# Last output blocks of each sublayer: four blocks per token half at a time, in place of two

## The chip, the cores and the metric

The kernel runs on one core of a Trainium2 chip. The metric is the device time of one execution in microseconds; the time before is the median of three runs.

## The reference, cut to what matters

One inference step through two trunk layers, for 512 prompt tokens and 64 sample tokens that share all weights. Each layer has three sublayers: an FFN, a mixer, an FFN. Each sublayer normalises its input, ends in a matrix product onto 1024 outputs, normalises that, and adds it to the residual stream.

```python
def swiglu(x, w_gate, w_up, w_down):
    return (jax.nn.silu(x @ w_gate) * (x @ w_up)) @ w_down
...
        x = x + 0.5 * rmsnorm(swiglu(rmsnorm(x, g[0]), ffn_gate[li, 0], ffn_up[li, 0], ffn_down[li, 0]), g[1])
        h = rmsnorm(x, g[2])
...
        x = x + rmsnorm(y, g[3])
        x = x + 0.5 * rmsnorm(swiglu(rmsnorm(x, g[4]), ffn_gate[li, 1], ffn_up[li, 1], ffn_down[li, 1]), g[5])
```

The mixers are a gated DeltaNet beside a short convolution (even layer) and sparse attention beside a gating MLP (odd layer); both end in one output projection. A norm needs a sum over all 1024 outputs of a token, so a sublayer's result can be normalised for a token only when all of that token's output blocks are there.

## The kernel before, in words

Activations lie transposed: 128 features on the partitions, KC = 8 chunks of features, tokens along the free axis. The 576 tokens are split in two halves, half 0 with 256 columns and half 1 with 320 (`HW`). Every product is done in three passes (`mm3`): high part of the weight by high part of the activation, high by low, low by high. A weight tile is loaded by SP's queue (`raw`), its high part is cast by ACT (`whi`) and its low part subtracted on DVE (`wlo`); tiles rotate in a pool `wp` of four. TensorE (PE) is the engine that the layout is built for.

**The end of a sublayer.** `ffn` (its second part) and `proj_out` make eight output blocks `mb` for each half `hf`. A block of an FFN is 33 matmuls (11 chunks, three passes), one of an output projection 24. `self.out_order` sets their order: blocks 0 to 5 for half 0 and half 1 in turn, then blocks 6 and 7 for half 0, then 6 and 7 for half 1. When half 0 has its last block, `boundary` is called for it, and later for half 1.

**The boundary.** It has a chain of its own. The sum of squares of y (`acc`, kind y) is summed over partitions by two or three one-column matmuls (L161); ACT takes a root (L163), DVE a reciprocal (L167), PE spreads it by a transpose (L173). Then DVE scales y (L234, `bt`) and adds it to the residual x (L236, L238), ACT and DVE write the high and low part of the next sublayer's operand (L202 `xh`, L203 `xl`), ACT squares x (L186) and POOL adds the squares up (L187, `acc`, kind x). From that `acc` a second round of L161, L163, L167, L173 makes the next sublayer's pre-norm factor r. For half 0 that second round is written straight into the boundary; for half 1 it is put off (`later`) until the last chunk of the next sublayer's first group.

**The next sublayer.** Its first group has four weight tiles. `group` does all four for half 0, tile by tile, then all four for half 1 chunk by chunk. PSUM has five banks for them (three `g`, two `f`), so half 1 needs banks that DVE must first have emptied of half 0's results (in an FFN L316 and L317, tiles t and u; in the mixers L433, L472 and others).

**What sets the order.** The code records operations; a scheduler orders each engine's queue by its own estimate of times. At run time each engine takes its queue in that order, so an instruction that waits holds all behind it. Tiles of a pool that is opened anew wait for the tiles that lay at their address before (`reuse_waits="tile"`).

Of the kernel before, what the change touches and what calls it, by code (L numbers as in the profile page):

```python
# [8 lines left out]
F32 = mybir.dt.float32  # L9
F32R = mybir.dt.float32r  # L10
# [6 lines left out]
P = 128  # L17
# [6 lines left out]
KC = D // P  # L24
# [9 lines left out]
HW = (256, 320)  # L34
# [4 lines left out]
class Step:  # L39
    def __init__(self, ctx, tc, a, o):  # L40
# [17 lines left out]
        self.small = {}  # L58
        self.out_order = [(mb, hf) for mb in range(KC - 2) for hf in range(2)]
        self.out_order += [(mb, hf) for hf in range(2) for mb in range(KC - 2, KC)]  # L60

# [42 lines left out]

    def weight(self, src, inner=P, pool=None):
        nc = self.nc
        pool = pool or self.wp
        shape = [P, 8 * P // inner, inner]
        raw = self.wp.tile(shape, F32, tag="raw", name=self.nm("raw"), bufs=3)
        bufs = 4 if pool is self.wp else 2  # L110
        hi = pool.tile(shape, F32R, tag="whi", name=self.nm("whi"), bufs=bufs)
        lo = pool.tile(shape, F32R, tag="wlo", name=self.nm("wlo"), bufs=bufs)
        nc.sync.dma_start(raw, src)
        self.last_split = self.split(hi, lo, raw)
        return hi, lo
# [26 lines left out]
    def behind(self, inst):  # L142

        return self.tc.issue_after(inst.ins) if inst else nullcontext()

    def new_act(self):
        hi, lo = [], []
        for hf in range(2):
            hi.append(self.res.tile([P, KC, HW[hf]], F32R, tag=f"xh{hf}", name=self.nm("xh")))
            lo.append(self.res.tile([P, KC, HW[hf]], F32R, tag=f"xl{hf}", name=self.nm("xl")))  # L150
        return hi, lo

# [131 lines left out]
    def ffn(self, l, f, act, rs, gpost, gnext, first=None):  # L284
        nc, a = self.nc, self.a
        with ExitStack() as ctx:
            hp = ctx.enter_context(self.tc.tile_pool(name=self.nm("ffn"), bufs=1, reuse_waits="tile"))
            yp = ctx.enter_context(self.tc.tile_pool(name=self.nm("y"), bufs=1, side="right", reuse_waits="tile"))
            y = [yp.tile([P, KC, HW[hf]], F32, name=self.nm("y")) for hf in range(2)]
            accy = [None, None]  # L290
            nact, nrs = None, [None, None]
            rs = list(rs)
            hp.tile([P, 16], F32, tag="pad", name=self.nm("pad"))
            for part in range(2):
# [26 lines left out]
                tiles = {}  # L321
                if part == 1:
                    x = self.load_x(yp)
                    if (l, f) == (0, 1):
                        nc.sync.dma_start(self.o["win_past"], a["win"])
                    if (l, f) == (0, 0):
                        self.small_weights()

                def block(n):
                    t = n // 8  # L330
                    if t not in tiles:
                        tiles[t] = self.weight(a["wdn"][l, f, part, t], pool=yp if part == 1 and t >= 9 else None)
                    return tiles[t][0][:, n % 8, :], tiles[t][1][:, n % 8, :]

                for mb, hf in self.out_order:
                        w = HW[hf]
# [6 lines left out]
                        else:  # L343
# [4 lines left out]
                            if mb == KC - 1:  # L348
                                if nact is None and gnext is not None:
                                    nact = self.new_act()  # L350
                                nrs[hf] = self.boundary(hf, y, x, accy[hf], gpost, 0.5, gnext, nact)
# [3 lines left out]
    def proj_out(self, wsrc, oact, order, gpost, gnext):  # L355
        nc = self.nc
        with ExitStack() as ctx:
# [5 lines left out]
            x = self.load_x(hp)  # L363
            for mb, hf in self.out_order:
                    if mb not in ws:
                        ws[mb] = self.weight(wsrc[mb], pool=hp if mb >= KC - 2 else None)
                    whi, wlo = ws[mb]
# [1130 lines left out]
```

## Time and profile before

| | us |
|---|---|
| median of three runs (lowest, highest) | 2471.99 (2470.40, 2478.14) |
| the profiled execution | 2458.22 |
| its span | 2456.2 |
| its mean granted TensorE clock | 0.986 |
| PE busy | 2408.7 (98% of the span) |
| DVE, ACT, POOL busy | 1246.9, 925.6, 185.9 |

A granted clock of 1.00 is TensorE's upper level, 2.4 GHz, and 0.50 the lower, 1.2 GHz. The program has six sublayers in this order: FFN, even mixer, FFN, FFN, odd mixer, FFN; so five boundaries between sublayers and one end. The boundaries lie near 424 us (first, FFN to mixer), 816 (second, mixer to FFN), 1237 (third, FFN to FFN), 1663 (fourth, FFN to mixer) and 2011 (fifth, mixer to FFN).

### The profile page before, as it was taken

The numbers are of one execution on the slowest core, as the hardware profiler recorded it, in microseconds if no ns is written. First come the engines' busy times: TensorE is split into PE (matmuls) and PEld (weight loads), VectorE is DVE, ScalarE is ACT, GpSimd is POOL, SyncE is SP. The second block draws the span as 40 slices with busy tenths as digits, with TensorE's granted clock in tenths as the row PEclk, the third lists the DMA queues.
The fourth block names the chain that finished last, engine by engine and source line by source line (L and its number), as shares of the span: only waits on it lengthen the run. The fifth ranks groups of instructions, "written<-read, shape, count | busy, mean of one in ns | idle before, by whom it ended". The sixth has DMA issues, their size and how long they took to land.

```text
span 2456.2 us, 43363 instructions
## 1 busy us (share of the span) xinstructions
PE 2408.7 (98%) x18169; PEld 2319.2 (94%) x18169; DVE 1246.9 (51%) x2482; ACT 925.6 (38%) x1719; POOL 185.9 (8%) x274
## 2 busy tenths in 40 slices
PE   7999999999999999999999999999999999999998
PEld 7999999898999999999999999999867799999997
DVE  5432443767765654244465424446647646423444
ACT  5322334554423532233353223243346645222332
POOL 3000000400001200000020000004103001000000
PEclk9999999999999999999999999999989999999999
DMA  6222222311214332222233222234502123222221
GB/s 223 83 84 76 97 86 89 108 43 52 68 53 143 112 104 87 86 79 86 95 120 104 78 87 87 86 96 149 177 24 78 57 78 138 86 87 78 86 87 56
DMA packets 70323, 226.72 MB, mean 92 GB/s; under 512 B 11136, under 2 KB 17568, under 8 KB 70096
## 3 DMA queue, kind: packets, MB, share of 16 engines
q1 hardware_dynamic: 64288, 204.27, 24.7%
q0 software_dynamic: 5552, 19.57, 2.4%
q8 instruction: 143, 2.34, 0.4%
q14 instruction: 52, 0.43, 0.1%
q10 hardware_dynamic: 288, 0.11, 0.0%
HBM read 204.26 MB, written 20.72 MB: 92 GB/s over the span
## 4 chain that ended last, share of the span: by engine, by line
PE 76%; issue 17%; DVE 5%; ACT 1%; DMA 1%; POOL 0%; POOLq 0%; SPq 0%; DVEq 0%; ACTq 0%
PE psg L119 14%; PE psg L121 14%; PE psg L120 14%; PE psf L120 8%; PE psf L121 8%; PE psf L119 8%; PE psm L1206 1%; PE psm L494 1%; DVE xl L203 1%; PE psm L516 1%; PE psf L1248 1%; PE psg L1235 1%; PE psm L514 1%; DVE x L236 1%; DVE bt L234 1%
## 5 line engine op out<-in xcount | busy, mean ns | idle before, releaser
L119 PE MATMUL psg<-xh,whi 128*128 128x256 f32 (+1 forms) x2464 | 734.6, 298 | 12.4 <-ACT whi L101 10.2
L120 PE MATMUL psg<-xl,whi 128*128 128x256 f32 (+1 forms) x2464 | 733.9, 298 | 5.1 <-DVE xl L203 4.7
L121 PE MATMUL psg<-xh,wlo 128*128 128x256 f32 (+1 forms) x2464 | 730.7, 297 | 2.2 <-DVE wlo L102 2.1
L102 DVE TENSOR_TENSOR wlo<-raw,whi 128x1024 fp32r<-128x1024 f32 x330 | 405.5, 1230 | 353.1 <-ACT whi L101 351.7
L101 ACT CAST whi<-raw 128x1024 fp32r<-128x1024 f32 x330 | 345.5, 1050 | 554.4 <-PE psg L120 344.9
L119 PEld LDWEIGHTS psg<-xh,whi 128*128 128x128 f32 x2464 | 467.5, 190 | 16.6 <-ACT whi L101 10.5
L120 PEld LDWEIGHTS psg<-xl,whi 128*128 128x128 f32 x2464 | 467.1, 190 | 9.6 <-DVE xl L203 7.7
L121 PEld LDWEIGHTS psg<-xh,wlo 128*128 128x128 f32 x2464 | 467.0, 190 | 4.4 <-DVE wlo L102 2.7
L120 PE MATMUL psf<-xl,whi 128*128 128x320 f32 (+1 forms) x1280 | 376.4, 294 | 1.5 <-DVE xl L203 1.3
L119 PE MATMUL psf<-xh,whi 128*128 128x320 f32 (+1 forms) x1280 | 376.5, 294 | 0.5 <-ACT xh L202 0.3
L121 PE MATMUL psf<-xh,wlo 128*128 128x320 f32 (+1 forms) x1280 | 375.9, 294 | 0.3
L119 PE MATMUL psg<-hh,whi 128*128 128x256 f32 (+1 forms) x836 | 246.0, 294 | 0.0
L120 PE MATMUL psg<-hl,whi 128*128 128x256 f32 (+1 forms) x836 | 245.6, 294 | 0.0
L121 PE MATMUL psg<-hh,wlo 128*128 128x256 f32 (+1 forms) x836 | 245.5, 294 | 0.0
L120 PEld LDWEIGHTS psf<-xl,whi 128*128 128x128 f32 x1280 | 240.7, 188 | 2.6 <-DVE xl L203 2.2
L119 PEld LDWEIGHTS psf<-xh,whi 128*128 128x128 f32 x1280 | 240.9, 188 | 1.2 <-ACT xh L202 0.5
L121 PEld LDWEIGHTS psf<-xh,wlo 128*128 128x128 f32 x1280 | 240.9, 188 | 0.9 <-DVE wlo L102 0.9
L187 POOL TENSOR_TENSOR acc<-acc,sq 128x320 f32<-128x320 f32 (+1 forms) x77 | 70.6, 917 | 1379.8 <-ACT sq L186 1358.8
L119 PE MATMUL psf<-hh,whi 128*128 128x320 f32 (+1 forms) x572 | 169.5, 296 | 0.0
L120 PE MATMUL psf<-hl,whi 128*128 128x320 f32 (+1 forms) x572 | 169.3, 296 | 0.0
L121 PE MATMUL psf<-hh,wlo 128*128 128x320 f32 (+1 forms) x572 | 169.0, 296 | 0.0
L101 ACT CAST hh<-u 128x320 fp32r<-128x320 f32 (+1 forms) x176 | 75.9, 433 | 243.4 <-DVE u L319 243.2
(469 smaller groups left out, 3192.8 us busy)
## 6 DMA issues: line engine op xcount, KB each, us to landing
raw<-in_wgu SPq DMA_DIRECT2D x176, 512.0 KB, 3.3
raw<-in_wdn SPq DMA_DIRECT2D x88, 512.0 KB, 3.3
raw<-in_w_ein SPq DMA_DIRECT2D x28, 512.0 KB, 3.4
raw<-in_w_oin SPq DMA_DIRECT2D x14, 512.0 KB, 3.5
xd<-x SPq DMA_DIRECT2D x10, 640.0 KB, 2.9
x<-xd POOLq DMA_DIRECT2D x10, 640.0 KB, 7.2
xd<-x SPq DMA_DIRECT2D x10, 512.0 KB, 2.7
x<-xd POOLq DMA_DIRECT2D x10, 512.0 KB, 5.0
```

Source lines behind the costliest of these rows:

```text
L101: first = nc.scalar.copy(hi, src)
L102: nc.vector.tensor_tensor(lo, src, hi.bitcast(F32), ALU.subtract)
L119: mm(out, whi, ahi, start=first, stop=False)
L120: mm(out, whi, alo, start=False, stop=False)
L121: mm(out, wlo, ahi, start=False, stop=last)
L187: return (eng or nc.vector).tensor_tensor(acc[:, :w], acc[:, :w], sq[:, :w], ALU.add)
L203: nc.vector.scalar_tensor_tensor(lo, xs, g, hi.bitcast(F32), ALU.mult, ALU.subtract)
L234: nc.vector.tensor_tensor(t, y[hf][:, k:k + n, :], r[:, None, :w].to_broadcast([P, n, w]), ALU.mult)
L236: (nc.gpsimd if gnext is None and hf and k == 0 else nc.vector).tensor_tensor(xs, xs, t, ALU.add)
L494: nc.tensor.matmul(pz[:w, i * w:i * w + w], m[:, i, :], x[:, i, :], start=True, stop=True)
L514: nc.tensor.matmul(pr[:, 1, i, :], xt[:, i, :], zt[:, i, :], start=True, stop=True)
L516: nc.tensor.matmul(pr[:, 0, i, :], zt[:, i, :], xt[:, i, :], start=True, stop=True)
```

## The change

`out_order` becomes a function: blocks 0 to 3 go in turn, then blocks 4 to 7 for one half, then 4 to 7 for the other. In the last sublayer half 1 goes first and half 0 last; elsewhere half 0 goes first. The first part of an FFN, which has no boundary behind it, goes in turn throughout (`in_turn`). The weights of the last four blocks are kept for both halves: in an output projection four tiles in its own pool (two before); in an FFN two in its pool and two in the room of half 1's operand of the sublayer that is ending (`spare`), whose last reader is done by then. Operand tiles are allocated half by half (`half_act`). The FFN's pad grows from 64 to 192 bytes. Line numbers shift: L161 becomes L171, L173 L183, L203 L213, L234 L244, L316 L326, L317 L327.

```diff
-        self.out_order = [(mb, hf) for mb in range(KC - 2) for hf in range(2)]
-        self.out_order += [(mb, hf) for hf in range(2) for mb in range(KC - 2, KC)]
+        self.in_turn = [(mb, hf) for mb in range(KC) for hf in range(2)]
+
+    def out_order(self, last):
+
+        halves = (1, 0) if last else (0, 1)
+        return [(mb, hf) for mb in range(KC - 4) for hf in halves] + [(mb, hf) for hf in halves for mb in range(KC - 4, KC)]
...
-    def weight(self, src, inner=P, pool=None):
+    def weight(self, src, inner=P, pool=None, bufs=2, dst=None):
...
-        bufs = 4 if pool is self.wp else 2
-        hi = pool.tile(shape, F32R, tag="whi", name=self.nm("whi"), bufs=bufs)
-        lo = pool.tile(shape, F32R, tag="wlo", name=self.nm("wlo"), bufs=bufs)
+        if dst:
+            hi, lo = dst
+        else:
+            bufs = bufs if pool else 4
+            hi, lo = [(pool or self.wp).tile(shape, F32R, tag=t, name=self.nm(t), bufs=bufs) for t in ("whi", "wlo")]
...
+    def half_act(self, hf):
+        return [self.res.tile([P, KC, HW[hf]], F32R, tag=f"x{s}{hf}", name=self.nm("x" + s)) for s in "hl"]
+
     def new_act(self):
...
+        return [list(t) for t in zip(*[self.half_act(hf) for hf in range(2)])]
+
+    def spare(self):
+
+        flat = [t.rearrange("p k c -> p (k c)")[:, 16:16 + 2 * KC * P].rearrange("p (i s c) -> p i s c", i=2, c=P)
+                for t in self.half_act(1)]
+        return [[t[:, i] for t in flat] for i in range(2)]
...
-            hp.tile([P, 16], F32, tag="pad", name=self.nm("pad"))
+            hp.tile([P, 48], F32, tag="pad", name=self.nm("pad"))
...
                 if part == 1:
+                    kept = self.spare()
                     x = self.load_x(yp)
...
-                        tiles[t] = self.weight(a["wdn"][l, f, part, t], pool=yp if part == 1 and t >= 9 else None)
+                        pool, dst = None, None
+                        if part == 1 and t >= 7:
+                            pool, dst = (yp, None) if t < 9 else (None, kept[t - 9])
+                        tiles[t] = self.weight(a["wdn"][l, f, part, t], pool=pool, dst=dst)
...
-                for mb, hf in self.out_order:
+                for mb, hf in self.out_order(gnext is None) if part else self.in_turn:
...
-                                if nact is None and gnext is not None:
-                                    nact = self.new_act()
+                                if gnext is not None:
+                                    nact[0][hf], nact[1][hf] = self.half_act(hf)
...
-            for mb, hf in self.out_order:
+            for mb, hf in self.out_order(False):
                     if mb not in ws:
-                        ws[mb] = self.weight(wsrc[mb], pool=hp if mb >= KC - 2 else None)
+                        ws[mb] = self.weight(wsrc[mb], pool=hp if mb >= KC - 4 else None, bufs=4)
```

**Where half 0's second round stands on PE.** The engine is PE, the place the third boundary, FFN to FFN. The `acc` in these rows is half 0's sum of squares of x (kind x). Before, in the next sublayer's first group (`psg` tiles of half 0 by the operand `xh`, `xl`):

```order
L119 MATMUL psg_13351<-xh_13084,whi_13328 128x256
L121 MATMUL psg_13376<-xh_13084,wlo_13335 128x256
L119 MATMUL psg_13376<-xh_13084,whi_13334 128x256
L120 MATMUL psg_13376<-xl_13085,whi_13334 128x256
L121 MATMUL psg_13376<-xh_13084,wlo_13335 128x256
L161 MATMUL psm_13154<-ones,acc_13097 128x1 x2
L119 MATMUL psg_13376<-xh_13084,whi_13334 128x256
```

In the changed kernel, still in the ending sublayer, in half 1's third block of the last four (`psf_13159`; `xh_12467` and `xl_12468` are kept weights here):

```order
L124 MATMUL psf_13159<-hh_11056,xh_12467 128x320
L125 MATMUL psf_13159<-hl_11058,xh_12467 128x320
L171 MATMUL psm_13070<-ones,acc_13013 128x1 x2
L126 MATMUL psf_13159<-hh_11056,xl_12468 128x320
L124 MATMUL psf_13159<-hh_11056,xh_12467 128x320
L125 MATMUL psf_13159<-hl_11058,xh_12467 128x320
L126 MATMUL psf_13159<-hh_11056,xl_12468 128x320
L124 MATMUL psf_13159<-hh_11056,xh_12467 128x320
L183 MATMUL psm_13076<-ident,rcol_13071 128x128 x2
```

From half 0's last output matmul to this sum there were 66 matmuls of 320 columns and 28 of 256 before; now there are 86 of 320 columns (at the first, fourth and fifth boundary too; 76 at the second).

**Where half 0's results leave PSUM.** The engine is DVE, the place the fifth boundary, odd mixer to the last FFN. `t` and `u` take half 0's first results out of PSUM; `bt`, `x` and `xl` belong to half 1's boundary chain. Before:

```order
L316 TENSOR_TENSOR t_21554<-psg_21504,r_21277 128x256
L236 TENSOR_TENSOR x_20743<-x_20743,bt_21352 128x640
L236 TENSOR_TENSOR x_20743<-x_20743,bt_21363 128x640
L203 SCALAR_TENSOR_TENSOR xl_21201<-x_20743,g,xh_21200 128x320
L234 TENSOR_TENSOR bt_21377<-y_20739,psm_21346 128x640
L317 TENSOR_TENSOR u_21555<-psg_21529,r_21277 128x256
L203 SCALAR_TENSOR_TENSOR xl_21201<-x_20743,g,xh_21200 128x320 x3
```

In the changed kernel:

```order
L244 TENSOR_TENSOR bt_21392<-y_20733,psm_21340 128x320
L213 SCALAR_TENSOR_TENSOR xl_21137<-x_20737,g,xh_21136 128x320
L248 SCALAR_TENSOR_TENSOR x_20737<-bt_21392,g,x_20737 128x320
L213 SCALAR_TENSOR_TENSOR xl_21137<-x_20737,g,xh_21136 128x320
L177 RECIPROCAL rcol_21645<-rcol_21645 128x2
L179 RECIPROCAL rcol_21645<-rcol_21645 64x1
L326 TENSOR_TENSOR t_21490<-psf_21440,r_21213 128x256
L326 TENSOR_TENSOR t_21548<-psg_21498,r_21213 128x256
L327 TENSOR_TENSOR u_21491<-psf_21465,r_21213 128x256
L327 TENSOR_TENSOR u_21549<-psg_21523,r_21213 128x256
```

All four now stand behind the whole of half 1's boundary chain and behind the reciprocal of its second round; the second boundary reads the same. In the built program the output projection's y of half 1 lies at bytes 167840 to 178080 of a partition and the FFN's t starts at 168288; before, y began at 176032 and t ended at 169440.

**What PE has to do meanwhile.** The engine is PE, the same place. Before, half 1's first group goes over its four tiles chunk by chunk from the start:

```order
L119 MATMUL psg_21562<-xh_21200,whi_21423 128x320
L119 MATMUL psf_21563<-xh_21200,whi_21429 128x320
L120 MATMUL psg_21562<-xl_21201,whi_21423 128x320
L121 MATMUL psg_21562<-xh_21200,wlo_21424 128x320
L120 MATMUL psf_21563<-xl_21201,whi_21429 128x320
L121 MATMUL psf_21563<-xh_21200,wlo_21430 128x320
L119 MATMUL psf_21564<-xh_21200,whi_21435 128x320
```

In the changed kernel the first tile goes alone through seven chunks (21 matmuls; its last two are the first rows here), then half 1's sum of x, its last chunk, the transpose, and only then the other three tiles:

```order
L125 MATMUL psg_21556<-xl_21137,whi_21417 128x320
L126 MATMUL psg_21556<-xh_21136,wlo_21418 128x320
L171 MATMUL psm_21644<-ones,acc_21344 128x1 x2
L171 MATMUL psm_21644<-ones,acc_21344 64x1
L124 MATMUL psg_21556<-xh_21136,whi_21417 128x320
L125 MATMUL psg_21556<-xl_21137,whi_21417 128x320
L126 MATMUL psg_21556<-xh_21136,wlo_21418 128x320
L183 MATMUL psm_21653<-ident,rcol_21645 128x128 x2
L183 MATMUL psm_21653<-ident,rcol_21645 128x64
L124 MATMUL psf_21557<-xh_21136,whi_21423 128x320
```

The number of matmuls, casts and DMAs is the same in both kernels.

## Rows read from the trace of the kernel before

**Rows 1.** The page's first part: busy us and share of each engine.

```profile
PE 2408.7 (98%) x18169; PEld 2319.2 (94%) x18169; DVE 1246.9 (51%) x2482; ACT 925.6 (38%) x1719; POOL 185.9 (8%) x274
```

**Rows 2.** Windows: stretch, length, busy PE PEld DVE ACT POOL, clock, DMA, GB/s.

```profile
60.00:424.00 364.00, 364.00 (x2785) 364.00 (x2784) 148.97 (x236) 111.70 (x178) 0.00 (x0) 1.00 0.27 88
424.00:470.00 46.00, 43.80 (x285) 42.23 (x284) 30.90 (x53) 22.00 (x48) 20.82 (x41) 0.89 0.29 97
...
824.00:864.00 40.00, 37.95 (x279) 35.99 (x279) 32.26 (x57) 24.40 (x51) 13.48 (x17) 1.00 0.37 134
...
1226.00:1264.00 38.00, 36.20 (x249) 34.77 (x248) 22.73 (x41) 15.63 (x34) 5.80 (x7) 0.91 0.19 70
...
1660.00:1690.00 30.00, 27.28 (x204) 25.75 (x204) 21.32 (x42) 12.93 (x31) 6.24 (x8) 1.00 0.19 64
...
2012.00:2056.00 44.00, 41.99 (x301) 39.49 (x300) 35.05 (x60) 27.02 (x58) 14.93 (x18) 1.00 0.31 116
```

**Rows 3.** Windows over the stretches with a low granted clock.

```profile
440.40:450.90 10.50, 10.50 (x48) 10.02 (x49) 4.27 (x11) 3.48 (x9) 5.82 (x15) 0.51 0.45 127
1253.40:1260.20 6.80, 6.80 (x35) 6.66 (x34) 2.95 (x6) 1.23 (x6) 0.63 (x1) 0.53 0.37 136
1771.50:1790.00 18.50, 17.83 (x70) 10.82 (x70) 10.79 (x56) 8.54 (x32) 0.00 (x0) 0.51 0.31 96
```

**Rows 4.** Timeline of PE, three block starts: start, duration, line, tiles, idle before.

```profile
411.30 0.31 PE L119 MATMUL psg<-hh,whi 128*128 128x320 f32 x1
...
416.14 0.28 PE L119 MATMUL psg<-hh,whi 128*128 128x256 f32 x1
...
420.03 0.28 PE L119 MATMUL psf<-hh,whi 128*128 128x256 f32 x1
```

**Rows 5.** Timeline at the third boundary, PE and POOL.

```profile
1236.80 0.31 PE L119 MATMUL psf<-hh,whi 128*128 128x320 f32 x1
...
1247.43 0.28 PE L119 MATMUL psg<-xh,whi 128*128 128x256 f32 x1
...
1253.24 0.79 POOL L187 TENSOR_TENSOR acc<-acc,sq 128x256 f32<-128x256 f32 x1 [1.27 <-ACT sq L186]
```

**Rows 6.** Timeline at the second boundary, PE, DVE and POOL.

```profile
816.17 0.31 PE L119 MATMUL psf<-xh,whi 128*128 128x320 f32 x1
...
818.90 1.28 DVE L234 TENSOR_TENSOR bt<-y,psm 128x512 f32<-128x512 f32 x2 [0.53 <-PE psm L173]
...
830.68 0.73 POOL L187 TENSOR_TENSOR acc<-acc,sq 128x256 f32<-128x256 f32 x1 [1.27 <-ACT sq L186]
```

**Rows 7.** Timeline at the fifth boundary, half 0, PE and POOL.

```profile
2011.35 0.31 PE L119 MATMUL psg<-xh,whi 128*128 128x320 f32 x1
...
2019.23 0.28 PE L119 MATMUL psf<-xh,whi 128*128 128x256 f32 x1
...
2027.26 0.73 POOL L187 TENSOR_TENSOR acc<-acc,sq 128x256 f32<-128x256 f32 x1 [1.27 <-ACT sq L186]
```

**Rows 8.** Timeline at the fifth boundary, half 1's chain, DVE, POOL and PE.

```profile
2032.30 1.55 DVE L234 TENSOR_TENSOR bt<-y,psm 128x640 f32<-128x640 f32 x2 [0.95 <-PE psm L173]
...
2045.95 1.07 POOL L187 TENSOR_TENSOR acc<-acc,sq 128x320 f32<-128x320 f32 x1 [0.36 <-ACT sq L186]
...
2048.61 0.71 PE L161 MATMUL psm<-ones,acc 128*128 128x1 f32 x6
...
2049.75 0.17 DVE L167 RECIPROCAL rcol<-rcol 128x2 f32<-128x2 f32 x1 [1.15 <-ACT rcol L163]
```

**Rows 9.** Timeline of PE in the odd mixer: the end of one wait.

```profile
1771.15 1.14 PE L999 MATMUL psm<-gt,sel_pair 64*128 64x24 f32 x7 [2.25 <-issue]
```

**Rows 10.** Timeline of DVE at the program's end, half 0 and half 1.

```profile
2436.93 1.28 DVE L234 TENSOR_TENSOR bt<-y,psm 128x512 f32<-128x512 f32 x2 [1.82 <-PE psm L173]
...
2446.82 1.55 DVE L234 TENSOR_TENSOR bt<-y,psm 128x640 f32<-128x640 f32 x2 [0.59 <-PE psm L173]
...
2452.29 1.01 DVE L238 SCALAR_TENSOR_TENSOR x<-bt,g,x 128x320 f32<-128x320 f32 x2
```

More of the change, by code (lines that the diff above doesn't have):

```diff
@@ L103, in split @@
         return first
-    def weight(self, src, inner=P, pool=None):
+    def weight(self, src, inner=P, pool=None, bufs=2, dst=None):
         nc = self.nc
-        pool = pool or self.wp
         shape = [P, 8 * P // inner, inner]
         raw = self.wp.tile(shape, F32, tag="raw", name=self.nm("raw"), bufs=3)
-        bufs = 4 if pool is self.wp else 2
-        hi = pool.tile(shape, F32R, tag="whi", name=self.nm("whi"), bufs=bufs)
-        lo = pool.tile(shape, F32R, tag="wlo", name=self.nm("wlo"), bufs=bufs)
+        if dst:
[3 more added lines that the diff above has]
+            hi, lo = [(pool or self.wp).tile(shape, F32R, tag=t, name=self.nm(t), bufs=bufs) for t in ("whi", "wlo")]
         nc.sync.dma_start(raw, src)
@@ L144, in behind @@
         return self.tc.issue_after(inst.ins) if inst else nullcontext()
+    def half_act(self, hf):
+        return [self.res.tile([P, KC, HW[hf]], F32R, tag=f"x{s}{hf}", name=self.nm("x" + s)) for s in "hl"]
     def new_act(self):
[L147 to L151, printed above, removed]
+        return [list(t) for t in zip(*[self.half_act(hf) for hf in range(2)])]
[3 more added lines that the diff above has]
+        return [[t[:, i] for t in flat] for i in range(2)]
     def rstd(self, acc, w, scale, eps, tag, bank="m"):
@@ L290, in ffn @@
             accy = [None, None]
-            nact, nrs = None, [None, None]
+            nact, nrs = [[None, None], [None, None]], [None, None]
             rs = list(rs)
-            hp.tile([P, 16], F32, tag="pad", name=self.nm("pad"))
+            hp.tile([P, 48], F32, tag="pad", name=self.nm("pad"))
             for part in range(2):
```

## The prediction

> **What bounds the kernel now.** I read the page's first part before anything else: PE is busy for 2408.7 us, 98% of the span, DVE for half of it, ACT and POOL for less [rows 1]. So the time is PE's work, its waits, and what it loses at the lower clock. Windows then show where the waits are. In the body of an FFN PE is busy for all of 364 us at clock 1.00; at each boundary between sublayers it is not: 46.00 - 43.80 = 2.20 us of waiting at the first, 2.05 at the second, 1.80 at the third, 2.72 at the fourth, 2.01 at the fifth, together 10.8 us [rows 2]. Behind two of the five the granted clock lies at about 0.5, the lower level: 10.50 us at 0.51 at the first, which cost 10.50 x 0.49 = 5.1 us against the upper level, and 6.80 us at 0.53 at the third, which cost 3.2; 8.3 together [rows 3]. At the second, fourth and fifth it stayed at 1.00 [rows 2]. The change adds and removes no matmul, cast or DMA, so it can only touch these 10.8 + 8.3 us and the end of the program.
>
> **The pace.** A block of 33 matmuls goes from 411.30 to 416.14 with 320 columns, 4.84/33 = 0.1467 us each, and from 416.14 to 420.03 with 256, 0.118 each [rows 4].
>
> **Term 1: half 0's second round.** What decides is when half 0's sum of squares of x is ready, and how much work PE has before the matmul that reads it; this matmul stands in PE's queue, and everything behind it waits. The sum is ready, counted from the start of the half 1 matmul that follows half 0's last output matmul, when POOL's last add ends. At the third boundary: 1253.24 + 0.79 - 1236.80 = 17.2 us [rows 5]; I take it for the three boundaries behind an FFN's output. At the second: 830.68 + 0.73 - 816.17 = 15.24 [rows 6]. At the fifth: 2027.26 + 0.73 - 2011.35 = 16.64 [rows 7]. ACT's, DVE's and POOL's steps of this chain are the same in the changed order, so I keep these lengths.
>
> PE's work until then in the changed order is 86 matmuls of 320 columns (76 at the second boundary), as the section on the change shows, plus the first round's sum and transpose for half 0. Those cost what the stretch of before lasts beyond its matmuls: 1247.43 - 1236.80 - 66 x 0.1467 = 0.94 at the third [rows 5], and at the fifth, with 48 matmuls, 2019.23 - 2011.35 - 7.05 = 0.83 [rows 7], which I use at the second too. So PE is at the sum after 86 x 0.1467 + 0.94 = 13.56 us at the first, third and fourth, 76 x 0.1467 + 0.83 = 11.99 at the second, 13.45 at the fifth. It waits 17.2 - 13.56 = 3.6 (three times), 15.24 - 11.99 = 3.25, and 16.64 - 13.45 = 3.19: 17.2 us together. The cover is no longer than before: at the third 66 matmuls of 320 columns and 28 of 256 took 9.69 + 3.30 + 0.94 = 13.93. The two more output blocks of half 1 are there, but the sum was moved up in front of most of them: when PE meets it, 13 matmuls of half 1's third block and the whole fourth are still to come (46 of 320 columns, 6.7 us), and these would have covered the wait. Half 1's own first round adds some 0.2 us a boundary of idle around its small matmuls, 1.0 in all, an estimate from the 0.8 to 0.9 above.
>
> What goes away for it: PE no longer meets half 0's operand before it is written, since half 0's chain is over when the next sublayer begins. So I strike all 10.8 us of waits of before.
>
> **Term 2: the first group behind a mixer.** At the second and fifth boundary the `t` and `u` of half 0's first group now stand on DVE behind half 1's whole chain and the reciprocal of its second round. Half 1 needs their banks. Count from T, the end of half 1's last output block. From there to half 1's first `bt` I take 3.2 us: for half 0 at the second boundary it is 818.90 - 816.17 = 2.73 [rows 6], and half 1 has a third piece of 64 tokens in the root and the reciprocal. From the first `bt` to the last add of squares it is 2045.95 + 1.07 - 2032.30 = 14.7 us; `t` and `u` stood between then, for which I take off 0.7 (an estimate, half of one `bt`), so 14.0; from the sum to the reciprocal's end 2049.75 - 2048.61 + 0.3 = 1.4 [rows 8]. So evictions begin near T + 18.6, and with some 0.9 for the first of them (an estimate, half of the 1.55 of a two-chunk `bt` and a little) half 1's second tile has its bank near T + 19.5. PE's work until it needs that bank: 96 matmuls of 256 columns (11.3 us), the small ones (0.83), a first tile of 24 matmuls of 320 columns (3.5), and the second round's sum and transpose (1.3): T + 17.0. So 2.5 us of waiting at each, 5.0 together. No row shows this order. The bounds are 1 us, if PE meets the sum itself late and part of this is the same wait, and 3 us.
>
> **The end of the program.** Half 0 now ends it. From the first `bt` to the last x half 1 needed 2452.29 + 1.01 - 2446.82 = 6.5 us; the same `bt` takes 1.28 for half 0 and 1.55 for half 1, a ratio of 0.83 [rows 10], so 1.1 us is saved, and some 0.3 in the steps ahead of it: -1.4. Half 1's chain has four blocks of half 0 as cover, 4 x 3.89 = 15.6 us, and lies beside it.
>
> **Edits that I cost at nothing.** The last two kept weights are written into half 1's old operand. Their first use is in block 6, behind at least four blocks for both halves, 4 x (4.84 + 3.89) = 35 us [rows 4] after its last reader, so the write waits for nobody. The output projection keeps four tiles in place of two: its pool casts the same number. Some loads of the next sublayer stand on SP behind half 0's stores; PE wants what they bring only in the next sublayer's first group, behind half 1's blocks. The pad and the allocation by halves move addresses alone. If one of these covers fails, a cast late by its own length costs some 1 us, once a sublayer (an estimate by DVE's operations of 1.0 to 1.6 us [rows 10]): up to +6, and it is no gain in any case.
>
> **The clock.** PE's waits of before came in pieces, 1.8 to 2.7 us a boundary, and behind two of five the clock fell. The one place elsewhere with a contiguous wait of such a size is in the odd mixer: 2.25 us of idle ended at 1771.15 [rows 9], and from 1771.50 the clock was 0.51 [rows 3]. The new waits are in one piece, 3.2 to 3.6 us, and two boundaries get a second one. So I let the clock fall at four of the five, at the mean of what it cost before, (5.1 + 3.2)/2 = 4.15 us: 16.6, that is +8.3 against before. The bounds are no fall at all (-8.3) and five falls of 5.1 (+17).
>
> The Trainium skill, "TensorE: Matmul & The Clock Gate", section "Part 1: The HAM clock gate", says that the default state is the throttled one and activity releases it, and that the cost varies from run to run. Read strictly, each boundary's wait would cost the clock: an estimate of five falls, 20.75 - 8.3 = +12.5, and the sum below would be 2495. The trace agrees in part: it fell at two boundaries of five. By that share there would be no change of clock and the sum would be 2483.
>
> **The sum.** Waits 17.2 + 1.0 + 5.0 = 23.2 for 10.8: +12.4. Clock +8.3. End -1.4. Together +19.3. On the profiled execution that is 2458.2 + 19.3 = 2477.5. That execution lies 13.8 us below the median of the three runs; I see no reason for the change to alter this distance, so on the median's scale it is 2472.0 + 19.3 = 2491.
>
> **The rivals.**
> A, the forecast: the wait for the sum moves into half 1's blocks and the clock falls at two to five boundaries: 2480 to 2506. Chance 0.62.
> B: the same waits, but the clock falls at one boundary or none. 2472.0 + 12.4 - 1.4 - 8.3 = 2474.7, or 2478.8 with one fall. For it speaks that three boundaries of before kept the clock through 2.0 to 2.7 us of waiting; against it, the one-piece wait of rows 9. Chance 0.14.
> C, the other side: half 0's chain is shorter in the changed kernel, because its DVE and ACT steps stand among fewer other ones, and the sum is ready when PE comes to it. The point is a chain of 13.5 us (12.0 at the second boundary) in place of 15.2 to 17.2. Then the waits and low clocks of boundaries go: -10.8 - 8.3 + 1.0 - 1.4 = -19.5, 2452; with the waits of term 2 left, 2457. For it speaks the end of the program, where the chain's `bt` to x takes only 6.5 us without operands to write [rows 10]; against it, that the steps are the same, one by one. Chance 0.18.
> D: the kept weights or the moved loads make PE wait as well, or the clock falls at more than one wait of a boundary: beyond 2506. Chance 0.06.
>
> **How the numbers follow.** A is the likeliest, so 2491. The range goes to 2506, A's upper end, and down to 2456, which takes in B and about half of C; left out are some 0.09 and 0.06. A measurement of this kernel can tell about 0.3%, 7.4 us, from no change: 2464.6 to 2479.4. Slower are A and D, 0.68; the same is B, 0.14; faster is C, 0.18.
>
> **What would show it.** In the profile of the changed kernel: at every boundary one wait of about 3 us on PE for POOL's `acc`, in the middle of half 1's third last block (the fourth at the second boundary); no wait for `xh` or `xl` as the next sublayer starts; at the second and fifth a wait of 1 to 3 us released by DVE's `t` or `u`; a granted clock near 0.5 behind most of these; some 1.4 us less from PE's last matmul to the end. It is wrong if PE reaches the sum with no wait (C), if the waits are there and the clock stays up (B), or if PE waits inside the last blocks for a kept weight (D).

## The result and the profile after

| | before | changed |
|---|---|---|
| median (lowest to highest of five) | 2471.99 us (2470.12 to 2478.14) | 2489.56 us (2485.80 to 2496.34) |
| the profiled execution | 2458.22 us | 2493.35 us |

The ratio is 1.0078, with a 95% interval of 1.0061 to 1.0094: 17.6 us slower, where 19 were forecast (2491). The page of the changed kernel answers [rows 1]:

```profile
PE 2422.6 (97%) x18169; PEld 2333.3 (94%) x18169; DVE 1244.1 (50%) x2482; ACT 917.8 (37%) x1715; POOL 183.6 (7%) x274
```

The longest PE waits, as a list of line, releaser, total, times and longest one, hold a new row, and the waits for `xl` (L213 here) and for the boundary's `xh` (L212) are gone from it:

```profile
PE psm L171 <- POOL acc L197: 19.0, 7, 3.1
```

Seven times PE waits at L171, the sum of squares over partitions, for POOL's `acc`. Five are half 0's second round, inside half 1's last blocks; two are half 1's second round, in the next sublayer's first group. This is the timeline at the second and the fifth boundary (start, duration, line, tiles, idle before), first half 0's sum in the middle of half 1's last block. Then, at the fifth, come PE's first matmul behind half 1's last block, half 1's sum behind 21 matmuls of the first tile with POOL's last add ahead of it, and DVE's rows behind that one:

```profile
820.50 0.30 PE L124 MATMUL psf<-xh,whi 128*128 128x320 f32 x1
823.89 0.80 PE L171 MATMUL psm<-ones,acc 128*128 128x1 f32 x3 [3.08 <-POOL acc L197]
...
2053.94 0.41 PE L124 MATMUL psf<-xh,whi 128*128 128x256 f32 x1
...
2070.28 0.31 PE L126 MATMUL psg<-xh,wlo 128*128 128x320 f32 x1
2072.14 0.86 POOL L197 TENSOR_TENSOR acc<-acc,sq 128x320 f32<-128x320 f32 x1 [1.45 <-ACT sq L196]
2073.05 1.31 PE L171 MATMUL psm<-ones,acc 128*128 128x1 f32 x6 [2.47 <-POOL acc L197]
...
2074.84 0.16 DVE L179 RECIPROCAL rcol<-rcol 64x1 f32<-64x1 f32 x1
2074.92 0.40 DVE L326 TENSOR_TENSOR t<-psf,r 128x256 f32<-128x256 f32 x1
```

The first kind of wait is 2.65 us at the three boundaries behind an FFN and 3.08 and 3.05 at the two behind a mixer; the second kind stands at the two behind a mixer alone, 2.47 us at each. The next windows answer [rows 2 and 3] (length, busy PE PEld DVE ACT POOL, granted clock, DMA share, GB/s). The first four run at the first, second, third and fifth boundary, each from the same matmul to the same matmul of the program as the stretches of before that the table below gives; the others are the places where the granted clock is low.

```profile
414.40:464.65 50.25, 47.43 (x325) 46.44 (x323) 32.29 (x56) 23.40 (x50) 20.88 (x41) 0.93 0.26 92
799.52:866.52 67.00, 61.35 (x428) 59.56 (x426) 38.70 (x70) 28.95 (x69) 15.19 (x18) 0.92 0.23 88
1225.83:1282.32 56.49, 53.73 (x378) 52.74 (x376) 35.82 (x64) 25.86 (x56) 13.33 (x16) 0.94 0.16 62
2029.39:2096.34 66.95, 61.43 (x428) 59.72 (x426) 41.51 (x73) 29.87 (x69) 15.19 (x18) 0.92 0.27 98
...
431.10:437.90 6.80, 6.28 (x25) 6.24 (x26) 3.50 (x7) 2.42 (x7) 0.46 (x1) 0.50 0.34 127
823.70:830.40 6.70, 6.51 (x26) 6.47 (x26) 1.63 (x4) 2.04 (x7) 0.13 (x1) 0.50 0.09 35
850.90:854.30 3.40, 3.40 (x14) 3.40 (x14) 3.14 (x8) 3.37 (x8) 1.65 (x4) 0.51 0.72 202
1250.30:1257.10 6.80, 6.80 (x27) 6.76 (x28) 3.85 (x7) 2.37 (x6) 0.00 (x0) 0.50 0.26 92
1677.00:1683.70 6.70, 6.70 (x27) 6.66 (x28) 3.92 (x7) 2.37 (x6) 0.00 (x0) 0.50 0.23 86
2052.50:2055.80 3.30, 3.30 (x16) 3.30 (x15) 1.27 (x3) 1.96 (x6) 0.00 (x0) 0.50 0.01 2
2073.00:2079.70 6.70, 6.64 (x25) 6.13 (x26) 4.50 (x12) 4.84 (x10) 2.13 (x4) 0.50 0.57 195
```

The clock fell at all seven waits, during the wait or within 2 us of its end: 40.4 us at half rate. The table has the length in us of the same stretches in every kernel, from each profile; the last column is the odd mixer (about 1640 to 1800 us), fourth boundary included.

| kernel | first | second | third | fifth | odd mixer |
|---|---|---|---|---|---|
| before | 50.0 | 60.0 | 55.1 | 60.1 | 160.0 |
| changed | 50.3 | 67.0 | 56.5 | 67.0 | 181.2 |
| e1_sum_later | 44.2 | 63.1 | 50.2 | 64.8 | 154.2 |
| e2_mixers_two | 47.4 | 60.0 | 55.9 | 60.1 | 160.6 |
| e3_both | 44.2 | 59.9 | 50.2 | 59.9 | 155.8 |
| e4_fill | 49.2 | 68.8 | 55.2 | 67.7 | 159.3 |
| e5_changed_again | 49.8 | 67.2 | 55.0 | 68.5 | 177.9 |
| e6_fill_right | 50.1 | 64.1 | 56.4 | 65.4 | 176.0 |
| e7_before_sum_later | 46.2 | 59.8 | 52.4 | 59.6 | 175.3 |
| e8_end_only | 45.6 | 60.3 | 54.1 | 60.0 | 177.0 |

The 21 us of the odd mixer are not the change's doing, as the last two rows show: see e5_changed_again. The first boundary's 50.0 us of before hold the longest fall of the clock of [rows 3]. That fall does not come in every execution: e8_end_only leaves this boundary as it was before, and there the clock stayed up.

```profile
416.63:462.25 45.62, 43.40 (x324) 41.99 (x323) 33.43 (x56) 23.08 (x49) 19.33 (x31) 1.00 0.33 107
```

### The profile page after: what moved, and what is told of

It is laid out like the page before. It is cut to its first block, busy times and chain, and to the rows that moved or that the text cites. A ratio compares the mean times of both kernels' runs of the same rounds, so it can differ in the third digit from the quotient of the medians.

```text
span 2491.3 us, 43355 instructions
## 1 busy us (share of the span) xinstructions
PE 2422.6 (97%) x18169; PEld 2333.3 (94%) x18169; DVE 1244.1 (50%) x2482; ACT 917.8 (37%) x1715; POOL 183.6 (7%) x274
## 4 chain that ended last, share of the span: by engine, by line
PE 92%; DVE 5%; issue 1%; ACT 1%; DMA 0%; POOL 0%; another core or an unknown queue 0%; POOLq 0%; ACTq 0%; SPq 0%; DVEq 0%
PE psg L124 17%; PE psg L125 17%; PE psg L126 17%; PE psf L126 10%; PE psf L125 10%; PE psf L124 10%; PE psm L1220 1%; DVE xl L213 1%; PE psm L508 1%; PE psm L530 1%; PE psf L1262 1%; PE psg L1249 1%; PE psm L528 1%; PE psm L171 1%; DVE x L246 1%
## 5 line engine op out<-in xcount | busy, mean ns | idle before, releaser
L124 PE MATMUL psg<-xh,whi 128*128 128x320 f32 (+1 forms) x2464 | 734.3, 298 | 10.6 <-ACT whi L105 10.6
L126 PE MATMUL psg<-xh,wlo 128*128 128x320 f32 (+1 forms) x2464 | 731.4, 297 | 2.0 <-DVE wlo L106 2.0
L125 PE MATMUL psg<-xl,whi 128*128 128x320 f32 (+1 forms) x2464 | 732.9, 297 | 0.0
L106 DVE TENSOR_TENSOR wlo<-raw,whi 128x1024 fp32r<-128x1024 f32 x322 | 396.6, 1233 | 315.3 <-ACT whi L105 314.1
L125 PE MATMUL psg<-hl,whi 128*128 128x320 f32 (+1 forms) x766 | 226.1, 295 | 0.0
L124 PE MATMUL psg<-hh,whi 128*128 128x320 f32 (+1 forms) x766 | 226.1, 295 | 0.0
L126 PE MATMUL psg<-hh,wlo 128*128 128x320 f32 (+1 forms) x766 | 225.8, 295 | 0.0
L124 PE MATMUL psf<-hh,whi 128*128 128x256 f32 (+1 forms) x514 | 149.7, 291 | 0.0
L126 PE MATMUL psf<-hh,wlo 128*128 128x256 f32 (+1 forms) x514 | 149.7, 291 | 0.0
L125 PE MATMUL psf<-hl,whi 128*128 128x256 f32 (+1 forms) x514 | 149.7, 291 | 0.0
```

The costliest lines, as they stand in the source:

```text
L106: nc.vector.tensor_tensor(lo, src, hi.bitcast(F32), ALU.subtract)
L124: mm(out, whi, ahi, start=first, stop=False)
L125: mm(out, whi, alo, start=False, stop=False)
L126: mm(out, wlo, ahi, start=False, stop=last)
```

## Experiments

The medians of before were 2453.8 us beside the first four runs and 2470.6 beside the other four, so kernels are compared by their ratio to the kernel before on the same chip. The changed kernel stands at 1.0078.

**e1_sum_later: the sum behind half 1's last block.**

```diff
-            return later if hf else later()
+            return later
...
                             if mb == KC - 1:
...
+                                if hf == 1 and callable(nrs[0]):
+                                    with self.tc.issue_after(self.last_mm.ins):
+                                        nrs[0] = nrs[0]()
```

(`last_mm` is the last matmul written so far; `proj_out` gets the same lines.)

> The changed kernel with one thing moved: half 0's second round (the sum of squares of x, its root, reciprocal and transpose) stands on PE behind the last matmul of half 1's last output block, at all five boundaries, not inside half 1's third or fourth block. My theory (the wait on PE for POOL's acc is 2.7 to 3.1 us at each of five boundaries because the sum stands too early, and the granted clock falls behind it): the sum is ready when PE gets to it at the three boundaries behind an FFN (PE there at about 20 us, the sum ready at 17) and nearly so behind the mixers, so some 13 of 14.3 us of waits go, and with them the falls of the clock at the first, third and fourth boundary (6.8 us each at half rate, 3.4 us each); the second wait at the second and fifth boundary (2.5 us each) stays. About 2465 us. The rival (half 0's chain bounds the boundary wherever its sum stands, the wait turns up as waits for xh, xl, t or u): 2485 to 2492.

Measured: 0.9972 of the kernel before (0.9960 to 0.9983); 2465 was 0.9972. PE at the third boundary passes the sum without a wait, then goes straight on; the window of this boundary stands below it, and that of the second:

```profile
1248.27 0.31 PE L126 MATMUL psf<-hh,xl 128*128 128x320 f32 x1
1248.42 0.50 PE L171 MATMUL psm<-ones,acc 128*128 128x1 f32 x4
1248.78 0.36 PE L124 MATMUL psg<-xh,whi 128*128 128x256 f32 x1
```

```profile
794.36:857.50 63.14, 59.93 (x427) 57.91 (x426) 38.90 (x70) 29.00 (x69) 15.24 (x18) 0.95 0.26 94
1220.10:1270.28 50.18, 50.13 (x378) 49.61 (x376) 36.00 (x64) 26.02 (x56) 14.40 (x17) 1.00 0.20 73
```

PE is busy for 50.13 of 50.18 us at clock 1.00. So behind an FFN half 0's chain does fit beside four blocks, and nothing else is late there: the place of the sum made the wait. Behind the mixers, whose blocks have 24 matmuls in place of 33, the second wait and a low clock stay, and at the fifth boundary a part of the first wait too (0.18 us are left of it at the second):

```profile
2009.59 0.60 PE L171 MATMUL psm<-ones,acc 128*128 128x1 f32 x4 [1.62 <-POOL acc L197]
```

**e2_mixers_two: output projections as before.**

```diff
-            for mb, hf in self.out_order(False):
+            for mb, hf in self.in_turn[:2 * KC - 4] + [(mb, hf) for hf in range(2) for mb in range(KC - 2, KC)]:
...
-                        ws[mb] = self.weight(wsrc[mb], pool=hp if mb >= KC - 4 else None, bufs=4)
+                        ws[mb] = self.weight(wsrc[mb], pool=hp if mb >= KC - 2 else None)
```

> The changed kernel with its output projections as before: two blocks half by half, two kept weights, the pool 16 KB smaller; the FFNs keep four. My theory (the output projection's larger pool is what puts t and u behind half 1's chain, and with the early sum costs 5.7 + 5.5 us of waits at the second and fifth boundary against 2.0 each before, and 10.2 us each at half clock): t and u stand between half 1's first steps again, those waits are 2 us each, the clock does not fall there; 7 + 10 us less, about 2473 us. The rival (the second wait of 2.5 us at these boundaries comes from half 1's chain alone, whatever the pool): the first wait goes and the second stays, about 2480 us.

Measured: 0.9996 (0.9987 to 1.0005), where 2473 was 1.0004 and the rival's 2480 1.003. The second boundary is 60.03 us long at clock 1.00, as before, and L171's wait for POOL's `acc` is down from 19.0 to 8.7 us:

```profile
796.29:856.32 60.03, 57.95 (x427) 55.72 (x426) 39.42 (x68) 31.38 (x69) 15.01 (x18) 1.00 0.31 115
```

```profile
PE psm L171 <- POOL acc L197: 8.7, 5, 2.9
```

Both waits behind the mixers go with the two extra blocks there, the second one too. The edit takes away the extra blocks and the larger pool together, so it cannot tell which of the two made the second wait. The three waits behind the FFNs stay, and at the first boundary the clock did not fall behind the same 2.65 us at which it fell in the changed kernel:

```profile
431.27 0.61 PE L171 MATMUL psm<-ones,acc 128*128 128x1 f32 x4 [2.65 <-POOL acc L197]
```

```profile
414.07:461.42 47.35, 44.60 (x324) 43.65 (x323) 32.18 (x56) 23.40 (x50) 20.88 (x41) 1.00 0.28 98
```

That stretch is 2.9 us shorter than in the changed kernel's first profile, with the same wait in it.

**e3_both: the two edits together.** No further edit.

> Both edits: half 0's second round behind half 1's last output block, and the output projections as before with two blocks. Behind the FFNs the cover is four blocks. My theory: the three boundaries behind an FFN lose their waits (2.2, 1.8 and 2.7 us before, 2.7 to 2.8 in the changed kernel) and their low clock; the two behind a mixer are as before, 2 us each, or up to 3 us longer where the sum now stands two blocks behind half 0 and is not ready; the end of the program keeps its 1.9 us. About 2453 to 2460 us, faster than the kernel before. The rival (waits turn up elsewhere): 2472 or more.

Measured: medians of 2434.07 against 2453.79 us; the ratio over all runs is 0.9925 (0.9912 to 0.9937). It beats both kernels. The first, second and third boundary:

```profile
414.58:458.76 44.18, 44.13 (x325) 43.61 (x323) 31.54 (x56) 23.34 (x50) 22.15 (x41) 1.00 0.32 113
793.64:853.50 59.86, 57.79 (x428) 55.68 (x426) 39.46 (x68) 31.39 (x69) 14.79 (x18) 1.00 0.30 115
1212.86:1263.05 50.19, 50.14 (x377) 49.63 (x376) 36.03 (x64) 26.03 (x56) 14.41 (x17) 1.00 0.20 72
```

The boundaries behind an FFN have no wait left and no low clock; against before's profile, the first is 5.8 us shorter and the third 4.9, falls of the clock included (against e8_end_only's, 1.4 and 3.9). Those behind a mixer are as before. This is what the four blocks can give where the sum stands behind them.

**e4_fill: unused matmuls in the wait.**

```diff
+            if hf == 0:
+                p, h6 = self.psum("m"), act[0][0][:, 6, :]
+                for _ in range(24):
+                    nc.tensor.matmul(p[:, :w], h6[:, 0:P], h6, start=True, stop=True)
             return later if hf else later()
```

> The changed kernel with 24 more matmuls of 256 columns (2.8 us) right ahead of half 0's second sum at each of the five boundaries; their result is not used. They need the seventh chunk of half 0's new operand, which is written at 1246.3 at the third boundary, before PE comes to them at 1247.4. So PE's wait there is filled with work and the sum comes no earlier. My theory (the wait itself costs its 2.7 to 3.1 us, and the idle time brings the clock down behind it): the waits shrink to a few tenths, no time is lost to the extra matmuls, and the low clock behind these five waits goes: up to 30.7 us at half rate, 15 us less, about 2474 to 2480 us. The rival (the clock falls for another reason, or the low stretches cost nothing since PE waits anyway): 2488 to 2492 us.

Measured: 1.0070 (1.0055 to 1.0084), outside the 1.0008 to 1.0032 that 2474 to 2480 stood for, and inside the rival's 1.0065 to 1.0081. The time alone does not decide, since the edit did more than was meant: the scheduler put the sum and its filling 11 to 15 matmuls earlier in half 1's blocks, so that these matmuls, cover before, now stand behind the sum. At the third boundary the sum still runs 24.4 us behind the start of the stretch, as in the changed kernel; at the second, half 0's operand wasn't yet written when PE came to the filling:

```profile
1251.36 3.13 PE L263 MATMUL psm<-xh 128*128 128x256 f32 x24 [0.41 <-ACT xh L212]
1255.22 0.61 PE L171 MATMUL psm<-ones,acc 128*128 128x1 f32 x4 [0.73 <-POOL acc L197]
```

```profile
820.64 4.34 PE L263 MATMUL psm<-xh 128*128 128x256 f32 x24 [2.07 <-ACT xh L212]
```

Behind the FFNs the trace speaks for the theory. The waits are down to 0.41 and 0.73 us, and the clock stayed at 1.00 at all three boundaries, where it fell at all three in both profiles of the changed kernel. The third:

```profile
1230.83:1286.06 55.23, 53.87 (x401) 52.49 (x400) 35.92 (x64) 25.97 (x56) 13.31 (x16) 1.00 0.17 64
```

Its length shows no gain: 55.2 us, against 56.5 and 55.0 in the changed kernel's two profiles.

**e5_changed_again: the changed kernel beside the next three.**

> The changed kernel once more, unaltered, beside the two that follow and on the same chip. In its first profile the stretch around the fourth boundary and the odd mixer's start holds about 20 us in which several engines wait for nothing that the profile names, and the three edited kernels before have none of it there. My theory (the change costs its five first waits, two second waits and the low clock behind them, and the 20 us are not its doing): 1.0078 of the kernel before again, within 0.15%, the boundaries as in the first profile, and the odd mixer within 3 us of the kernel before. The rival (the 20 us belong to the change): they are there again.

Measured: 1.0079 (1.0062 to 1.0097). The seven waits are there again, 18.6 us in all. But the odd mixer's long stretch is there too, so by what was written the rival has it. The two kernels behind it speak against the rival: they are the kernel before but for one edit each, and on the same chip their odd mixer is as long (175.3 and 177.0 us, against 160.0 in before's first profile). One window of it, in e7_before_sum_later here and in e1_sum_later from the other chip, over the same matmuls:

```profile
1704.41:1810.05 105.64, 90.93 (x550) 77.41 (x550) 48.71 (x137) 34.00 (x70) 18.79 (x20) 0.82 0.43 136
```

```profile
1701.79:1789.77 87.98, 84.67 (x550) 73.40 (x550) 48.56 (x137) 33.25 (x68) 16.62 (x17) 0.88 0.48 157
```

So these 15 to 21 us are not the change's. In the table they go with the chip: the four kernels of the first chip have 154.2 to 160.6 us there, the four of the second 175.3 to 177.9. They would also account for the 13.8 us between before's profiled execution and its median, if those came from two such chips; this is not on record.

**e6_fill_right: the filling at the sum's own place.**

```diff
-            return later if hf else later()
+            if hf:
+                return later
+            def filled(n):
+                p, h = self.psum("m"), act[0][0][:, 2, :]
+                for _ in range(n):
+                    nc.tensor.matmul(p[:, :w], h[:, 0:P], h, start=True, stop=True)
+                return later()
+            return filled
...
+                            if callable(nrs[0]) and hf == 1 and mb == KC - 2 and k == 6:
+                                with self.tc.issue_after(self.last_mm.ins):
+                                    nrs[0] = nrs[0](22)
...
+                        if callable(nrs[0]) and hf == 1 and mb == KC - 1 and n == 2:
+                            with self.tc.issue_after(self.last_mm.ins):
+                                nrs[0] = nrs[0](26)
```

> The changed kernel with half 0's sum held at the place where it stands there (behind the seventh chunk of half 1's third block in an FFN, behind the third of its fourth block in a mixer) and 22 (FFN) or 26 (mixer) unused matmuls of 256 columns ahead of it, 2.6 and 3.1 us, which need only the third chunk of half 0's operand, long written. So the first waits are filled with work of their own length and nothing is moved. My theory (idle time brings the clock down): sums at the same times as in the changed kernel, waits there under 0.7 us, no low clock behind them; 3.4 us less at each of the five, about 15 us, at the least 10: 0.996 to 0.994 of the changed kernel. The rival (the low clock comes whatever PE does there, or costs nothing): within 0.2% of the changed kernel.

Measured: 1.0054 (1.0039 to 1.0069). The median is 2481.97 us beside the 2488.99 of e5_changed_again on the same chip: 7 us less, between the 10 of the theory and the rival's 5, and with six runs each it does not tell the two apart. The trace does, place by place. Behind the mixers the theory holds: the filling runs right up to the sum (at the fifth a wait of 0.68 us is left), no clock falls behind it, and the boundaries are 64.1 and 65.4 us for 67.2 and 68.5. At the second:

```profile
822.12 3.28 PE L266 MATMUL psm<-xh 128*128 128x256 f32 x26
825.24 0.50 PE L171 MATMUL psm<-ones,acc 128*128 128x1 f32 x4
```

Behind the FFNs the wait at the sum went and the next one took its place: the transpose, which the edit holds behind the sum too, waits for a reciprocal that DVE has behind two weight casts (1.43 to 1.46 us). At the first and third boundary the clock falls there. The third, and its clock ahead of that wait and behind it:

```profile
1251.35 0.61 PE L171 MATMUL psm<-ones,acc 128*128 128x1 f32 x4
...
1254.54 0.40 PE L183 MATMUL psm<-ident,rcol 128*128 128x128 f32 x2 [1.43 <-DVE rcol L177]
```

```profile
1248.60:1254.50 5.90, 4.51 (x35) 4.15 (x33) 5.79 (x11) 2.92 (x7) 1.42 (x2) 1.00 0.33 115
1254.90:1258.30 3.40, 3.40 (x15) 3.40 (x14) 0.98 (x2) 0.84 (x2) 0.00 (x0) 0.51 0.63 219
```

At the fourth about the same wait left the clock up:

```profile
1681.09 0.40 PE L183 MATMUL psm<-ident,rcol 128*128 128x128 f32 x2 [1.45 <-DVE rcol L177]
```

```profile
1681.00:1690.00 9.00, 8.85 (x64) 8.68 (x65) 2.08 (x5) 1.72 (x5) 0.00 (x0) 1.00 0.47 127
```

So at the second boundary, where PE was kept busy and the second wait (2.1 us) and its fall were as in e5_changed_again, the clock stayed up and 3.1 us came back. At the fifth a part of the 3.0 us is a shorter fall behind the second wait. Behind the FFNs the filling gained nothing: the first and third stretch are 50.1 and 56.4 us for 49.8 and 55.0.

**e7_before_sum_later: the kernel before with the sum later.** Two blocks per half; half 0's second round behind the second tile of the next first group.

```diff
-            ps = [self.proj(t, act, hf, bank=self.bank()) for t in ws]
-            rs[hf] = rs[hf]()
+            ps = []
+            for t in ws:
+                ps.append(self.proj(t, act, hf, bank=self.bank()))
+                if len(ps) == (4 if self.first_group else 2):
+                    with self.tc.issue_after(self.last_mm.ins), self.urgent(not self.first_group):
+                        rs[hf] = rs[hf]()
```

> The kernel before, two blocks half by half, with only half 0's second round moved: behind the second tile of half 0's first group in the next sublayer. My theory (with two blocks of half 1 as cover PE meets half 0's operand before it is written, and the four blocks are what removes that): the waits for the sum go (3.3 us in all before), those for xh and xl stay or grow, so 0.997 to 1.001 of the kernel before, well short of e3_both's 0.9925. The rival (the place of the sum is all, the four blocks add nothing): 0.994 or less.

Measured: 0.9996 (0.9985 to 1.0007), no difference. PE still waits for half 0's operand:

```profile
PE psg L121 <- DVE xl L209: 4.8, 9, 1.1
...
PE psg L120 <- ACT xh L208: 2.3, 4, 0.7
```

So at the boundaries behind an FFN the later sum alone gives nothing (0.9996), four blocks alone give nothing (e2_mixers_two, 0.9996), and together they gain (e3_both, 0.9925). It is the four blocks at the mixers as well that make the changed kernel slower than before (1.0078).

**e8_end_only: the order of halves at the end, with two blocks.**

```diff
-                for mb, hf in self.out_order:
+                for mb, hf in [(mb, hf if gnext is not None or part == 0 else 1 - hf) for mb, hf in self.out_order]:
```

> The kernel before with one thing changed: in the last sublayer half 1 goes first and half 0 last, two blocks each. My theory: from PE's last matmul to the end 8.5 us in place of 9.7, and from the last y-sum on 0.8 us less, together 1.4 to 2.0 us; nothing else differs. The rival (half 1's chain lies now beside half 0's with only two blocks between and delays it): no gain or a loss.

A miss; the rival has it. The one run gave 2470.72 us beside a median of 2470.63, which alone tells nothing of 2 us; the trace shows the end itself later. PE waits 4.04 us for half 0's sum of y, because DVE takes half 0's last results out of PSUM (L344) only when half 1's chain is through:

```profile
2458.35 0.98 PE L161 MATMUL psm<-ones,acc 128*128 128x1 f32 x4 [4.04 <-DVE acc L187]
```

```profile
2449.91 1.55 DVE L234 TENSOR_TENSOR bt<-y,psm 128x640 f32<-128x640 f32 x2 [1.91 <-PE psm L173]
...
2455.43 1.01 DVE L238 SCALAR_TENSOR_TENSOR x<-bt,g,x 128x320 f32<-128x320 f32 x2
2456.35 0.75 DVE L344 TENSOR_TENSOR y<-psg,y 128x256 f32<-128x256 f32 x2
```

With four blocks half 1's chain is over in time, and nothing delays the changed kernel's last chain. First and last row on DVE, it takes 2488.03 + 0.49 - 2483.25 = 5.3 us against the 6.5 of [rows 10]; half 0's last chain is as short in e8_end_only, but starts late there:

```profile
2483.25 1.28 DVE L244 TENSOR_TENSOR bt<-y,psm 128x512 f32<-128x512 f32 x2 [0.85 <-PE psm L183]
...
2488.03 0.49 DVE L248 SCALAR_TENSOR_TENSOR x<-bt,g,x 128x256 f32<-128x256 f32 x1
```

## Why the prediction was right, step by step

- **Term 1, half 0's sum.** Right in place and mechanism: one wait at each boundary, released by POOL's `acc`, where the order had put the sum; e1 took it away behind the FFNs and at the second boundary, and half of it at the fifth, by moving the sum alone. That the remaining blocks would have covered the wait was worked out for the third boundary and is right there; at the fifth they cover it only in part. Forecast 3.6 behind an FFN, measured 2.65: the chain there came out about 1 us shorter than in [rows 5]. From the start of the y-sum to that of the x-sum it is 14.7 us in the changed kernel and 15.6 in before. The step "I keep these lengths" held behind the mixers (3.25 and 3.19 forecast, 3.08 and 3.05 measured) and was a little too long behind the FFNs.
- **The waits struck out.** Right: no wait for `xl` or for the boundary's `xh` is left.
- **Term 2.** The size and the two places came out, 2.5 us forecast and 2.47 measured; the mechanism did not, and the close number is in part luck. PE waits there for POOL's `acc`, at half 1's sum, and not for DVE's `t` or `u` and a bank for the second tile. The text had this case only as a bound, although the order shown before it has the sum behind 21 matmuls of the first tile. By the prediction's own terms half 1's sum is ready at T + 3.2 + 14.0 = T + 17.2 and PE is there at T + 11.3 + 0.8 + 3.1 = T + 15.2. At the fifth boundary, with T at 2053.94, both came later: ready at T + 19.1 (2072.14 + 0.86), PE there at T + 16.7, the clock at half for part of the way. `t` and `u` follow the reciprocal at once (2074.92), as the order showed, and no wait for a bank is left. e2 shows that this wait belongs to the extra blocks and the larger pool of the output projections. That `t` and `u` stand late because that pool reaches into the addresses of the FFN's pool, and that this in turn put the sum so early, is argued from the built program alone and not shown.
- **The small waits of half 1's first round.** 1.0 us was too much. The boundaries' waits are 19.6 us in all, of which the seven named ones make 19.0: +8.8 against before, not +12.4.
- **The clock.** Right in kind, undersized: four falls of 4.15 us were chosen, and there were seven of 2.9, at all five boundaries and twice behind the mixers. 40.4 us at half rate are 20.2 lost, +11.9 against the 8.3 of before where +8.3 stood. The prediction's reading of the Trainium skill's page "TensorE: Matmul & The Clock Gate" ("Part 1: The HAM clock gate"), that every such wait costs the clock, was nearer here than the two in five of [rows 3], but not exact: in e2 the first boundary's 2.65 us did not. The Trainium skill's page itself speaks there of longer idle gaps than any of the seven waits, so the reading went beyond it and the runs decide. The cost varies from run to run, as the Trainium skill's page says: behind the wait at the third boundary 6.8 us in one execution of the changed kernel and 3.4 in the other. e6 shows the cause at the second boundary, where a filled wait kept the clock, and e4 agrees behind the FFNs.
- **The end.** -1.4 forecast; the chain on DVE is 1.2 us shorter, and that it starts in time rests on the four blocks (e8).
- **The sum.** 8.8 + 11.9 - 1.2 = +19.5 by these rows, +19.3 forecast, +17.6 measured. The waits were oversized by 3.6 and the clock undersized by as much, so the closeness of the total is partly luck. Some of the low clock lies beside waits and costs less than its half; the stretches of the first, second, third and fifth boundary are 0.2 + 7.0 + 1.4 + 6.9 = 15.5 us longer, and the fourth, over the same 333 matmuls (1640.02 to 1687.13 before, 1647.60 to 1697.00 changed), 2.3: with the end, 16.6 together. The base matters as well: against e8's profile, whose clock fell at the second, third and fourth boundary, the same four stretches are 20.6 us longer.
- **The 13.8 us between profile and median** were carried over unexplained. The change did not touch them, as the ratio of 1.0079 on the second chip bears out. That they lie in the odd mixer and go with the chip (above) is likely and not shown.
- **The kept weights and loads** cost nothing: the only waits of PE for a weight's cast, 10.6 and 2.0 us, stand at the program's start and were there before (10.2 and 2.1).

Rival C did not come about, but e1 and e3 show how near it was behind the FFNs: the cover was there, and only half 0's sum in PE's queue stood ahead of it.

## What to carry to other kernels

More independent work behind a chain hides it only if no reader of that chain stands in the same queue ahead of that work: look in the built order for where the reader lands, and hold it behind the cover by hand where the scheduler's estimate is short. Change the place of the reader and the amount of cover together, since here either alone gave nothing. Keeping more buffers can change the order of the next stage, so look there too before counting the gain. Price a PE wait with the low clock that often follows.

## What was not expected of the hardware

- The length of a single wait did not settle whether the granted clock fell. It fell behind 1.43 us at the third boundary of e6_fill_right and stayed at 1.00 behind 1.45 at the fourth. Of the nine waits of 2.6 to 2.9 us for half 0's sum behind an FFN (the changed kernel's two profiles and e2_mixers_two) it fell at eight, and at the first boundary of e2_mixers_two it did not. It also stayed at 1.00 through 2.05 us of waiting in pieces at the second boundary of before [rows 2].
- Two chips gave the kernel before 2453.8 and 2470.6 us as medians. In the profiles from the slower one the odd mixer takes 15 to 18 us more than the 160.0 of before's, where gathers from DRAM are issued and PE waits up to 4.6 us with no releaser named. What delays them is open.
